# Ranks by due time instead of program place in a kernel's list scheduler (hybrid attention layer, one core)

## The chip, the cores and the metric

One core of one Trainium2 chip. The metric is device time in microseconds (us) of one execution. A kernel's engines are TensorE (PE, with its weight loads PEld), ScalarE (ACT), VectorE (DVE), GpSimd (POOL) and SyncE (SP), which issues all the DMA transfers of this kernel. Each engine works through its own list of instructions strictly in the order in which they were emitted, and waits on semaphores for what other engines or transfers have to deliver.

## The reference

One layer of a streaming encoder for two groups with the same weights: a prompt of 1024 rows and a sample of 32 rows with a cache of 512 positions. Cut to what matters:

```python
u = rmsnorm(h, g_pre) @ w_in                  # (1024, 4096): qA kA vA gA qB kB vB gB
oA = band_attention(qA, kA, vA)               # 8 heads of 64: own 64-frame chunk and 8 before, position bias, softmax
oB = stick_breaking(qB, kB, vB)               # 8 heads of 64: strictly causal
y = concat(oA * silu(gA), oB * silu(gB)) @ w_out
h = h + rmsnorm(y, g_post)
h = h + sigmoid(h @ w_ple_gate) * (p @ w_ple)
# stick_breaking:
log_1m = where(causal, log_sigmoid(-z), 0.0)
after = cumsum(log_1m, reverse=True) - log_1m
w = where(causal, exp(log_sigmoid(z) + after), 0.0)
```

The keys and values are outputs too. All is float32; matrix products are made of three products of rounded high and low parts (names ending in h and l).

## The kernel before, in words

The program is not written engine by engine. Code in program order records each instruction as an `Op` in a `Recorder` (`rec`), with its engine, its costs (`busy`: how long it occupies the engine, `late`: how long its result takes after that) and the instructions it has to come after (`after`: data, reuse of buffers). `Recorder.order` then plays a list schedule through in planned time, and `emit` writes the instructions in that order. This order is what each engine later runs; planned times themselves leave no trace on the chip. All instructions come out at one source line (L452), so the profile is read by tile names.

In `order`, the engine that is free first takes, of the instructions whose inputs are ready by then, the one with the least `key`. Keys are set in `node`: for TensorE `(cls, place in the program)`, where attention has class 0 and the projections 1 (other classes at the end); for the other four engines `(low, place in the program)`, where `low` is 0 except for a few steps (-2 and -1 for norm chains, 1 for the weight sums on GpSimd). Entries with engine "CTL" take or release buffers and cost nothing. A transfer occupies SyncE for `ISSUE`, then a common `line` for its bytes, and lands after constants; a result that goes to TensorE gets `MARGIN` more.

The stages in time:

1. Start-up (to about 40 us): x tiles are loaded, normed (`be`, `rs`), transposed on TensorE (`ptx`) into `hnh`/`hnl`, with part of the per-layer embedding product (`ple`).
2. Attention (to about 610 us): eight pairs of heads, A0, B0, A1, B1 and so on. The input projection of the next pair (`mm_qA`, `mm_kB`, ...) is woven by `weave` between scores (`SA`, `SB`), weights and values (`PVA`, `PVB`) of the present one. Scores of B go through mask (DVE), sigmoid (ACT), a scan (DVE), a difference (POOL); those of A through bias and minimum (DVE) and Exp (ACT). Weights are then transposed, mostly on TensorE (`ptwA`, `ptwB`), for two blocks of a head by a transpose on VectorE and a trip through memory: a store `swapA<-om` and four reads `be<-swapA`; then a cast to `wTh` and a subtraction to `wTl`. Keys and values go out through `ktA`, `ktB`, `vtA`, `vtB`. In the first four pairs sums of weight quarters are made for later on GpSimd (`oB`, `gB`, stored to `sum_dro`, `sum_drg`). In the last pair the eight gate projections run (`mm_gA`, `mm_gB`).
3. Output and gate projections (to the end): seven products of quarter matrices (`o0P`, `g0P`, ...) per pair of row tiles, with norm, gate and stores.

Of the kernel before, what the change touches and what calls it, by code (L numbers as in the profile page):

```python
# [8 lines left out]
F32 = mybir.dt.float32  # L9
F32R = mybir.dt.float32r  # L10
AF = mybir.ActivationFunctionType
# [161 lines left out]


class Op:
    __slots__ = ("eng", "what", "args", "kw", "key", "busy", "late", "ready", "left", "after", "at", "size", "shared")


LAND = {"PE": 165, "ACT": 0, "DVE": 0, "POOL": 0, "SP": 0, "CTL": 0}
SEM = 60  # L180
MARGIN = 400
ISSUE = 600
DMA_NS, DMA_RATE, DMA_MARGIN = 1500, 320.0, 2000
DVE_SET, POOL_SET = 137, 110


# [77 lines left out]
class Recorder:  # L264
# [35 lines left out]
    def node(self, eng, what, args, kw, after):  # L300
        o = Op()
        o.eng, o.what, o.args, o.kw, o.after = eng, what, args, kw, after
        o.key = (self.cls if eng == "PE" else self.low, len(self.ops))
        o.shared = False
        self.ops.append(o)
        return o

    def add(self, eng, what, args, kw):
        writes, reads = [], []
        method = what[1] if isinstance(what, tuple) else ""  # L310
        for i, a in enumerate(args):
            if isinstance(a, (View, Raw, Segments)):
                (writes if i == 0 or (method == "tensor_tensor_reduce" and i == 7) else reads).append(a)
        for k, a in kw.items():
            if isinstance(a, (View, Raw, Segments)):
                (writes if k in ("out", "accum_out") else reads).append(a)
        o = self.node(eng, what, args, kw, set())
        for mine, write in ((reads, False), (writes, True)):
            for v in mine:
                b = v.buf  # L320
                hit = False
                for other, box, wrote in b.uses:
                    if other is not o and (write or wrote) and all(p < y and x < q for (p, q), (x, y) in zip(v.box, box)):
                        o.after.add(other)
                        hit = True
                if b.pool is not None:
                    if not hit:
                        o.after.add(b.place)
                    b.pool.ops.append(o)
                b.uses.append((o, v.box, write))  # L330
        o.busy, o.late = self.cost(eng, method, args, kw, writes, reads)
        o.shared = eng == "POOL"
        if eng == "DVE":
            sbuf = [v for v in reads if isinstance(v, (View, Segments)) and not v.buf.psum and v.free() > 4]
            o.shared = len(sbuf) > 1 or (method == "tensor_copy" and len(sbuf) == 1 and not writes[0].buf.psum)

    @staticmethod
    def cost(eng, method, args, kw, writes, reads):

        out = writes[0] if writes else None  # L340
        n = out.free() if isinstance(out, View) else 1
        psum = any(isinstance(v, (View, Segments)) and v.buf.psum for v in reads)
        if eng == "PE":
            if method == "transpose":
                return (109 if args[1].shape[0] > 64 else 62), 165
            return max(109.0, 2.5 + 0.449 * args[2].free()) * (1 if args[2].buf.dtype == F32R else 4), 165
        if eng == "ACT":
            return (60 if psum else 95) + 0.83 * n + (190 if "accum_out" in kw else 0), 105
        if eng == "DVE":
            if method == "tensor_tensor_scan":  # L350
                return 120 + 2.1 * n, 85
            if method == "tensor_copy" and not psum:
                return 70 + 0.53 * n, 85
            if method == "scalar_tensor_tensor":
                return 125 + 1.04 * n, 85
            if method == "tensor_tensor_reduce":
                return 90 + 1.04 * n, 150
            return 70 + 1.04 * n, 85
        if eng == "POOL":
            if method == "tensor_tensor":  # L360
                if n == 1:
                    return 535, 40
                return 170 + (1.77 if out.buf.dtype == F32 else 2.15) * n, 40
            if method == "tensor_scalar":
                return 255 + 0.86 * n, 0
            return 100 + 0.82 * n, 0
        size, run = 4, 0
        for v in (out, args[1]):
            if isinstance(v, View) and v.buf.pool is not None:
                size, run = 4 * v.shape[0] * v.free(), 4 * v.shape[-1]  # L370
        return ISSUE, max(size / DMA_RATE, size / run * (8.5 + 0.0365 * run) / 16)


    def order(self):

        import heapq
        for place, old in self.turns:
            place.after.update(x[0] for x in old.uses)
        users = {id(o): [] for o in self.ops}
        for o in self.ops:  # L380
            o.left, o.ready = len(o.after), 0.0
            for a in o.after:
                users[id(a)].append(o)
        names = ("PE", "ACT", "DVE", "POOL", "SP", "CTL")
        free = dict.fromkeys(names, 0.0)
        soon = {e: [] for e in names}
        now = {e: [] for e in names}
        for o in self.ops:
            if not o.left:
                heapq.heappush(soon[o.eng], (0.0, o.key, id(o), o))  # L390
        out, port, line = [], 0.0, 0.0
        while len(out) < len(self.ops):
            best = None
            for e in names:
                if now[e]:
                    t = free[e]
                elif soon[e]:
                    t = max(free[e], soon[e][0][0])
                else:
                    continue  # L400
                if best is None or t < best[0]:
                    best = (t, e)
            t, e = best
            while soon[e] and soon[e][0][0] <= t:
                _, key, n, o = heapq.heappop(soon[e])
                heapq.heappush(now[e], (key, n, o))
            o = heapq.heappop(now[e])[2]
            if o.shared and e == "DVE" and port > t + DVE_SET:
                held = [x for x in now[e] if not x[2].shared]
                if held:  # L410
                    heapq.heappush(now[e], (o.key, id(o), o))
                    pick = min(held)
                    now[e].remove(pick)
                    heapq.heapify(now[e])
                    o = pick[2]
            o.at = t
            if e == "CTL":
                done = t
            elif e == "SP":
                free[e] = t + o.busy  # L420
                line = max(line, t + o.busy + DMA_NS) + o.late
                done = line + DMA_MARGIN
            else:
                if o.shared:
                    t = max(t, port - (DVE_SET if e == "DVE" else POOL_SET))
                    port = t + o.busy
                free[e] = t + o.busy
                done = t + o.busy + o.late
            out.append(o)
            for u in users[id(o)]:  # L430
                if u.eng == e and e != "SP":
                    r = t if e == "CTL" else free[e] if e == "PE" else done
                else:
                    r = done + (0 if u.eng == "CTL" else SEM + (MARGIN if u.eng == "PE" else 0))
                u.ready = max(u.ready, r)
                u.left -= 1
                if not u.left:
                    heapq.heappush(soon[u.eng], (u.ready, u.key, id(u), u))
        return out


    def emit(self, tc):
# [15 lines left out]
def stream_step(  # L458
# [333 lines left out]
    def attention(ab, p, h):  # L792
# [23 lines left out]
        def rooms(i):  # L816

            more = ab == "B"
            g = together.get(i, (i,))
            if g not in whole:  # L820
                n = sum(cost(x) for x in g) * P
                whole[g] = ring0.tile([P, n + more * len(g)], f"om{nm}_{i}"), ring1.tile([P, n], f"be{nm}_{i}")
            k, n = g.index(i), cost(i) * P
            a = sum(cost(x) for x in g[:k]) * P
            w0, w1 = whole[g]
            return w0[:, a + more * k:a + more * k + n + more], w1[:, a:a + n]
# [886 lines left out]
    for m, (nm, src, group) in enumerate(sets):  # L1713
        last_set = m == len(sets) - 1
        state = [{}, {}]
        for n, prod in enumerate(ORDER):
            for pair, t in enumerate(group):
# [43 lines left out]
                if nm == "o":  # L1761
                    rec.low = -1
                    if prod == "P2":
                        add(st["h1u"][:, L], st["p1"], bank, ALU.add)
                        st["u"].square(0, st["h1u"][:, L])
# [103 lines left out]
```

## Time and profile before

| | us |
|---|---|
| median of 3 runs | 804.93 |
| lowest and highest run | 804.59, 805.31 |
| profiled execution, its own time | 809.23 |
| its span, first to last instruction | 807.4 |
| VectorE busy in it | 567.9 |
| ScalarE busy in it | 504.4 |
| GpSimd busy in it | 432.1 |

The profiled execution is one single run with recording on. Its span is what the views below divide up. In a view of waits a row names the waiting engine and tile, the engine and tile it waited for, and then the total in us, the number of times and the longest. In a timeline a row gives start, duration, engine, line, operation, output<-input, and in brackets idle time before it and what ended it. SPq is SyncE's queue of transfer issues; its duration is that of the issue and not of the transfer.

### The profile page before, as it was taken

To read this page: it belongs to the slowest core of one execution; us is meant where nothing else is said; L and a number is where in the kernel's file an instruction comes from. 1 tells how busy PE (TensorE), PEld (TensorE's weight loads), DVE (VectorE), ACT (ScalarE), POOL (GpSimd) and SP (SyncE) were. 2 spreads that over 40 slices of the span, in tenths; PEclk is the share of its full clock that TensorE was granted. 3 is DMA by queue.
4 is the path that set the end of the run, shared out by engine and by line. 5 is a ranking of instruction groups with operands and counts; after the bars stand their busy time and mean duration, and the time that the engine had idled before them with its cause. 6 is when DMAs were issued, how large, how long until landed. Compare 5 with 4: busy or idle time off the path is not lost.

```text
span 807.4 us, 14271 instructions
## 1 busy us (share of the span) xinstructions
PE 788.0 (98%) x4646; PEld 722.3 (89%) x4646; DVE 567.9 (70%) x1007; ACT 504.4 (62%) x1061; POOL 432.1 (54%) x503
## 2 busy tenths in 40 slices
PE   8999989999999999999999999999999999999997
PEld 7899989899989999899999989999997777878786
DVE  7626768786588788788886688765435787477655
ACT  5636774676586646795675696543327977877641
POOL 5623655764356668134551236777542549598513
PEclk9999999999999999999999999999999999999999
DMA  8419895667878749854535667765569948869633
GB/s 276 149 45 293 215 253 175 195 185 217 225 225 246 215 121 267 216 146 133 151 81 169 147 175 212 234 199 152 166 207 322 298 147 270 278 218 302 215 108 131
DMA packets 160973, 161.09 MB, mean 199 GB/s; under 512 B 39154, under 2 KB 120794, under 8 KB 160899
## 3 DMA queue, kind: packets, MB, share of 16 engines
q1 hardware_dynamic: 160898, 160.18, 67.1%
q8 instruction: 37, 0.61, 0.3%
q14 instruction: 38, 0.30, 0.1%
HBM read 99.23 MB, written 52.49 MB: 188 GB/s over the span
## 4 chain that ended last, share of the span: by engine, by line
PE 72%; DMA 6%; ACT 6%; POOL 5%; DVE 5%; issue 4%; SPq 2%; DVEq 0%; POOLq 0%; ACTq 0%
PE mm_gA L452 6%; PE mm_gB L452 6%; PE mm_kA L452 5%; PE mm_qA L452 5%; PE mm_qB L452 4%; PE SB L452 3%; PE mm_vA L452 3%; PE PVB L452 3%; PE mm_kB L452 3%; PE PVA L452 3%; PE mm_vB L452 3%; PE SA L452 2%; PE o1P L452 2%; PE g2P L452 2%; PE g3P L452 2%
## 5 line engine op out<-in xcount | busy, mean ns | idle before, releaser
L452 POOL TENSOR_TENSOR be<-om 128x128 f32<-128x128 f32 (+7 forms) x64 | 75.4, 1184 | 64.8 <-DVE om L452 29.0
L452 DVE TENSOR_TENSOR_SCAN om<-om,SB 128x384 f32<-128x384 f32 (+5 forms) x96 | 94.9, 1001 | 9.1 <-ACT om L452 7.4
L452 ACT ACTIVATE om<-SB 128x384 f32<-128x384 f32 (+5 forms) x96 | 44.4, 493 | 36.0 <-DVE SB L452 26.9
L452 ACT ACTIVATE be<-om,statA 128x640 f32<-128x640 f32 (+3 forms) x64 | 44.4, 694 | 18.2 <-DVE statA L452 11.0
L452 DVE TENSOR_TENSOR wTl<-be,wTh 128x640 fp32r<-128x640 f32 (+1 forms) x32 | 37.6, 1175 | 10.3 <-ACT wTh L452 8.8
L452 ACT CAST wTh<-ptwB 128x512 fp32r<-128x512 f32 (+3 forms) x64 | 29.5, 481 | 19.6 <-PE ptwB L452 15.4
L452 DVE TENSOR_TENSOR wTl<-ptwB,wTh 128x512 fp32r<-128x512 f32 (+3 forms) x64 | 33.7, 545 | 10.3 <-ACT wTh L452 7.8
L452 DVE TENSOR_TENSOR wTl<-ptwA,wTh 128x512 fp32r<-128x512 f32 (+2 forms) x64 | 29.8, 483 | 15.7 <-ACT wTh L452 12.5
L452 POOL TENSOR_TENSOR oB<-oB,oB 128x256 f32<-128x256 f32 x32 | 27.7, 882 | 18.6 <-DMA oB<-in_w_out_dram 10.5
L452 DVE STREAM_TRANSPOSE om<-be 128x640 f32<-128x640 f32 (+1 forms) x32 | 28.9, 904 | 9.8 <-POOL be L452 4.9
L452 PE MATMUL SB<-kdB,LB 128*128 128x384 f32 (+5 forms) x96 | 34.0, 357 | 1.6 <-DVE om L452 1.6
L452 DVE CUSTOM_DVE_ANT_0 om<-SA,biasA 128x320 f32<-128x320 f32 (+3 forms) x64 | 29.5, 482 | 7.6 <-PE SA L452 4.4
L452 ACT CAST wTh<-ptwA 128x512 fp32r<-128x512 f32 (+2 forms) x64 | 26.2, 426 | 13.3 <-PE ptwA L452 7.5
L452 PE MATMUL SB<-klB,LB 128*128 128x384 f32 (+5 forms) x96 | 32.9, 345 | 0.0
L452 PE MATMUL SA<-kdA,LA 128*128 128x320 f32 (+2 forms) x96 | 30.2, 325 | 0.7 <-DVE LA L452 0.4
L452 POOL TENSOR_TENSOR sggA<-sggA,oggA 128x352 f32<-128x352 f32 x24 | 23.8, 991 | 11.2 <-DVE sggA L452 10.8
L452 PE MATMUL SA<-klA,LA 128*128 128x320 f32 (+2 forms) x96 | 29.6, 320 | 0.0
L452 ACT CAST wTh<-be 128x640 fp32r<-128x640 f32 (+1 forms) x32 | 25.0, 782 | 6.4 <-DMA swapA<-om 3.3
L452 PE MATMUL ptwB<-ident,be 128*128 128x128 f32 x192 | 28.7, 273 | 0.0
L452 PE MATMUL ptwA<-ident,be 128*128 128x128 f32 x160 | 26.3, 276 | 2.0 <-ACT be L452 1.8
L452 DVE TENSOR_TENSOR SB<-SB,maskb 128x128 f32<-128x128 f32 x64 | 17.3, 287 | 13.5 <-PE SB L452 13.1
L452 POOL TENSOR_TENSOR klA<-stkA,kdA 64x1024 fp32r<-64x1024 f32 x8 | 20.7, 2587 | 8.2 <-ACT kdA L452 7.7
(707 smaller groups left out, 2650.5 us busy)
## 6 DMA issues: line engine op xcount, KB each, us to landing
swapA<-om SPq DMA_DIRECT2D x16, 320.0 KB, 2.8
be<-swapA SPq DMA_DIRECT2D x64, 80.0 KB, 3.9
oB<-in_w_out_dram SPq DMA_DIRECT2D x16, 256.0 KB, 4.9
sum_dro<-oB SPq DMA_DIRECT2D x16, 256.0 KB, 3.3
gB<-in_w_ple_gate_dram SPq DMA_DIRECT2D x16, 256.0 KB, 4.6
sum_drg<-gB SPq DMA_DIRECT2D x16, 256.0 KB, 3.8
x<-in_x_prompt_dram SPq DMA_DIRECT2D x16, 256.0 KB, 5.2
h_dr<-h SPq DMA_DIRECT2D x8, 512.0 KB, 3.3
```

Of the source, the lines that this page charges most:

```text
L452: getattr(getattr(tc.nc, o.what[0]), o.what[1])(*args, **kw)
```

## The change

`order` becomes a loop over two new functions. `plan` is the old list schedule; it now also returns when its last engine is free. `due` goes backwards through a plan: each instruction's due time is the earliest of what its users allow, TensorE instructions being due at the time at which the plan before had them; an instruction without users is due at the plan's end. Outside TensorE that due time becomes the `key`. One plan with the old keys is followed by three rounds of `due` and `plan`; the last plan is emitted (two conditions are switched off by `0`). TensorE keeps its key.

The cost constants change too: one wake-up time per engine instead of one margin for TensorE, 30 ns more for most instructions of ScalarE, VectorE and GpSimd, 520 instead of 600 ns for an issue, another landing time of transfers, and 1310 ns wherever ScalarE goes from Exp to Sigmoid or back.

```diff
-MARGIN = 400
-ISSUE = 600
-DMA_NS, DMA_RATE, DMA_MARGIN = 1500, 320.0, 2000
+WAKE = {"PE": 400, "ACT": 100, "DVE": 100, "POOL": 190, "SP": 0}
+ISSUE = 520
+DMA_RATE, LANDING, WAKE_DMA = 320.0, 2500, 200
+TABLE_NS = 1310
...
+        o.table = next((a for a in args if a in (AF.Exp, AF.Sigmoid)), None) if eng == "ACT" else None
...
-            return (60 if psum else 95) + 0.83 * n + (190 if "accum_out" in kw else 0), 105
+            return (90 if psum else 125) + 0.83 * n + (190 if "accum_out" in kw else 0), 105
...
-            return 70 + 1.04 * n, 85
+            return 100 + 1.04 * n, 85
...
     def order(self):
 
-        import heapq
         for place, old in self.turns:
             place.after.update(x[0] for x in old.uses)
         users = {id(o): [] for o in self.ops}
         for o in self.ops:
-            o.left, o.ready = len(o.after), 0.0
             for a in o.after:
                 users[id(a)].append(o)
+        best, end = self.plan(users)
+        for _ in range(3):
+            self.due(best, users, end)
+            out, last = self.plan(users)
+            if last >= end and 0:
+                break
+            best, end = out, last
+        return best
+
+    def due(self, out, users, end):
+
+        late, after = {}, {}
+        for o in reversed(out):
+            e = o.eng
+            t = after.get(e, end) if 0 and e != "CTL" else end
+            for u in users[id(o)]:
+                v = late[id(u)]
+                if u.eng == e and e not in ("SP", "CTL"):
+                    v -= 0.0 if e == "PE" else o.late
+                elif u.eng != "CTL":
+                    v -= SEM + WAKE[u.eng] + (WAKE_DMA if e == "SP" and u.eng != "SP" else 0) + o.late * (e != "SP")
+                elif e != "SP":
+                    v -= o.late
+                if e == "SP":
+                    v -= LANDING + o.late
+                t = min(t, v)
+            if e == "PE":
+                late[id(o)] = o.at
+                continue
+            late[id(o)] = t - o.busy if e != "CTL" else t
+            if e != "CTL":
+                after[e] = late[id(o)]
+                o.key = (late[id(o)], o.key[1])
+
+    def plan(self, users):
...
             elif e == "SP":
                 free[e] = t + o.busy
-                line = max(line, t + o.busy + DMA_NS) + o.late
-                done = line + DMA_MARGIN
+                line = max(line, free[e]) + o.late
+                done = line + LANDING
             else:
+                if o.table and o.table != table:
+                    table = o.table
+                    t = max(free[e] + TABLE_NS, t)
...
                 else:
-                    r = done + (0 if u.eng == "CTL" else SEM + (MARGIN if u.eng == "PE" else 0))
+                    r = done + (0 if u.eng == "CTL" else SEM + WAKE[u.eng] + (WAKE_DMA if e == "SP" and u.eng != "SP" else 0))
...
-        return out
+        return out, max(free.values())
```

More of the change, by code (lines that the diff above doesn't have):

```diff
@@ L175 @@
 class Op:
-    __slots__ = ("eng", "what", "args", "kw", "key", "busy", "late", "ready", "left", "after", "at", "size", "shared")
+    __slots__ = ("eng", "what", "args", "kw", "key", "busy", "late", "ready", "left", "after", "at", "size", "shared", "table")
 LAND = {"PE": 165, "ACT": 0, "DVE": 0, "POOL": 0, "SP": 0, "CTL": 0}
 SEM = 60
-MARGIN = 400
-ISSUE = 600
-DMA_NS, DMA_RATE, DMA_MARGIN = 1500, 320.0, 2000
+WAKE = {"PE": 400, "ACT": 100, "DVE": 100, "POOL": 190, "SP": 0}
+ISSUE = 520
+DMA_RATE, LANDING, WAKE_DMA = 320.0, 2500, 200
+TABLE_NS = 1310
 DVE_SET, POOL_SET = 137, 110
@@ L303, in node @@
         o.key = (self.cls if eng == "PE" else self.low, len(self.ops))
-        o.shared = False
+        o.shared, o.table, o.busy, o.late = False, None, 0.0, 0.0
         self.ops.append(o)
@@ L347, in cost @@
         if eng == "ACT":
-            return (60 if psum else 95) + 0.83 * n + (190 if "accum_out" in kw else 0), 105
+            return (90 if psum else 125) + 0.83 * n + (190 if "accum_out" in kw else 0), 105
         if eng == "DVE":
             if method == "tensor_tensor_scan":
-                return 120 + 2.1 * n, 85
+                return 150 + 2.1 * n, 85
             if method == "tensor_copy" and not psum:
-                return 70 + 0.53 * n, 85
+                return 100 + 0.53 * n, 85
             if method == "scalar_tensor_tensor":
-                return 125 + 1.04 * n, 85
+                return 155 + 1.04 * n, 85
             if method == "tensor_tensor_reduce":
-                return 90 + 1.04 * n, 150
-            return 70 + 1.04 * n, 85
+                return 120 + 1.04 * n, 150
+            return 100 + 1.04 * n, 85
         if eng == "POOL":
@@ L361, in cost @@
                 if n == 1:
-                    return 535, 40
-                return 170 + (1.77 if out.buf.dtype == F32 else 2.15) * n, 40
+                    return 565, 40
+                return 200 + (1.77 if out.buf.dtype == F32 else 2.15) * n, 40
             if method == "tensor_scalar":
@@ L380, in order @@
         for o in self.ops:
-            o.left, o.ready = len(o.after), 0.0
             for a in o.after:
                 users[id(a)].append(o)
+        best, end = self.plan(users)
[30 more added lines that the diff above has]
+    def plan(self, users):
+        import heapq
+        for o in self.ops:
+            o.left, o.ready = len(o.after), 0.0
         names = ("PE", "ACT", "DVE", "POOL", "SP", "CTL")
@@ L390, in order @@
                 heapq.heappush(soon[o.eng], (0.0, o.key, id(o), o))
-        out, port, line = [], 0.0, 0.0
+        out, port, line, table = [], 0.0, 0.0, None
         while len(out) < len(self.ops):
```

## The prediction

> **What bounds the kernel now.** I read the page's busy times first, then who TensorE (PE) waited for, then stretches around its worst wait, then SyncE's queue there.
>
> ```profile
> span 807.4 us, 14271 instructions
> PE 788.0 (98%) x4646; PEld 722.3 (89%) x4646; DVE 567.9 (70%) x1007; ACT 504.4 (62%) x1061; POOL 432.1 (54%) x503
> ...
> PE PVA L452 <- ACT wTh L452: 2.7, 1, 2.7
> PE ptx L452 <- DVE be L452: 2.4, 2, 1.3
> PE ptwA L452 <- ACT be L452: 1.8, 2, 1.3
> PE SB L452 <- DVE om L452: 1.6, 3, 0.9
> PE idle L452 <- DVE newh L452: 1.3, 1, 1.3
> PE ptkA L452 <- DVE wTl L452: 1.3, 1, 1.3
> PE ptx L452 <- DVE hnl L452: 0.5, 1, 0.5
> PE o0P L452 <- ACT A12o L452: 0.5, 1, 0.5
> ...
> PE g0P L452 <- DMA hh<-h_dr: 0.3, 1, 0.3
> ...
> 100.00:104.00 4.00, 1.35 (x9) 1.05 (x7) 0.24 (x1) 0.70 (x3) 2.65 (x3) 1.00 0.91 268
> 104.00:108.00 4.00, 3.92 (x14) 3.72 (x15) 3.11 (x4) 4.00 (x10) 1.74 (x5) 0.57 1.04 243
> 780.00:808.00 28.00, 22.48 (x109) 18.64 (x108) 13.80 (x23) 5.03 (x9) 6.46 (x5) 0.99 0.31 104
> ```
>
> TensorE is busy 788.0 of 807.4 us, so it is the bound, and an order of instructions can only touch the other 19.4 us. Of these, 1.3 us lie ahead of the first matmul (idle waiting for newh, the start-up), and the last stretch shows 28.00 - 22.48 = 5.5 us without a matmul, of which 0.6 lie behind the span's end: a tail of 4.9 us. About 13.2 us are left in the middle. The window rows read: stretch, busy time of PE, weight loads, DVE, ACT, POOL, then granted clock, DMA share and GB/s. The 2.7 us wait for wTh is followed by a stretch at clock 0.57, which costs (1 - 0.57) x 4.00 = 1.7 us of TensorE work more. So 13.2 + 1.7 = 14.9 us is all that a better order could win short of head and tail.
>
> The Trainium skill, page "TensorE: Matmul & The Clock Gate", section "Part 1: The HAM clock gate", says the clock halves after about one idle window of 3.4 us. By that figure a gap of 2.7 us would leave the clock alone and step A below would be worth 2.7 instead of 4.4, which gives 800.5 us; the row of 0.57 disagrees, and the row decides.
>
> Where that wait comes from is in SyncE's queue and in the ScalarE instruction that stood for it:
>
> ```profile
> 82.86 1.29 SPq L452 DMA_DIRECT2D swapA<-om  x1
> ...
> 88.03 0.47 SPq L452 DMA_DIRECT2D kdB<-kdB  x1
> 88.59 0.55 SPq L452 DMA_DIRECT2D out_dram<-ktB  x1
> 89.23 1.00 SPq L452 DMA_DIRECT2D out_dram<-vtA  x1
> 90.33 1.71 SPq L452 DMA_DIRECT2D klB<-klB  x1
> 92.09 3.06 SPq L452 DMA_DIRECT2D out_dram<-ktB  x3
> 95.20 0.94 SPq L452 DMA_DIRECT2D be<-swapA  x1
> 96.23 0.70 SPq L452 DMA_DIRECT2D oB<-in_w_out_dram  x1
> 96.98 0.43 SPq L452 DMA_DIRECT2D sum_dro<-oB  x1
> 97.46 0.96 SPq L452 DMA_DIRECT2D be<-swapA  x2
> ...
> 99.04 0.58 SPq L452 DMA_DIRECT2D be<-swapA  x1
> ...
> 103.31 0.72 ACT L452 CAST wTh<-be 128x640 fp32r<-128x640 f32 x1 [3.30 <-DMA swapA<-om]
> ```
>
> The block of weights was stored at 82.86, but the four reads that bring it back turned go out at 95.20 to 99.04, behind five output stores (ktB, vtA), two key copies and the traffic of the weight sums. Rank in the old plan is the place in the program (`key = (low, index)`), and these were written earlier. The cast starts at 103.31, and TensorE stands. The releaser is named swapA<-om, but the queue shows that the reads were late.
>
> **The change part by part.** No instruction is added or removed, and TensorE's own rank is untouched, so the 788.0 us stay. What changes is the order on ScalarE, VectorE, GpSimd and SyncE, and through the plan's ready times which ready matmul TensorE is given next.
>
> *A, due times on SyncE.* The reads be<-swapA have a user chain cast, subtract, PVA, whose due time is the matmul's time in the pass before. The output stores of ktB and vtA have none but the reuse of their buffer, or the end of the plan. The reads pass the seven transfers at 88.03 to 92.09 and the two of the sums at 96.23 and 96.98. What they pass: kdB and klB feed scores and have early due times themselves, so they may stay ahead; the five stores alone took 0.55 + 1.00 + 3.06 = 4.6 us of the queue, and the sum's two 0.70 + 0.43 = 1.1, together 5.7 us, more than the 2.7 of the wait. Behind the moved stores wait only later users of their buffer. I take the wait and its slow clock away: -4.4 (bounds 0 and -4.4).
>
> *B, due times on the compute engines.* Three waits inside the attention are of engines that did something else first: ptwA 1.8, SB 1.6, ptkA 1.3, together 4.7. The largest of ptwA is this:
>
> ```profile
> 472.30 1.28 ACT L452 ACT_TABLE_LOAD   x1
> 473.60 0.94 ACT L452 ACTIVATE om<-SB 128x128 f32<-128x128 f32 x3
> 474.55 1.28 ACT L452 ACT_TABLE_LOAD   x1
> 475.85 0.83 ACT L452 ACTIVATE be<-om,statA 128x640 f32<-128x640 f32 x1
> ```
>
> Sigmoids for the next head were put ahead of an exponential that the transposes waited for, with two table loads of 1.28 us that the old plan did not know. The new plan charges 1.31 for each and ranks the exponential by its due time. But it does not avoid a load, it only counts it, and both may be due closely. I take half: -2.3 (bounds 0 and -4.7).
>
> *C, start-up.* ptx 2.4 and 0.5, total 2.9. The chain to these transposes runs over ScalarE's square, GpSimd's root and VectorE's scaling of tiles that have just been loaded; how much of it is queue and how much transfer the wait rows do not tell, so I take a quarter, -0.7 (bounds +1.3, one more wait as long as the longest there, and -2.9). The rows of the last stage (o0P 0.5) and the tail I leave: after the last matmul the same chain of additions, gate and store has to run.
>
> *D, the new constants.* Each ScalarE, VectorE and GpSimd instruction counts 30 ns more, the wake-ups 100 to 190 ns more; this spreads the plan and costs nothing on the chip by itself. The allowance for a transfer shrinks. For 256 KB (0.82 at the plan's 320 bytes per ns) the old plan had 0.60 + 1.50 + 0.82 + 2.00 + 0.06 = 5.0 us from issue to user, the new one 0.52 + 0.82 + 2.50 + 0.26 = 4.1. Against that, issue to landing:
>
> ```profile
> be<-swapA SPq DMA_DIRECT2D x64, 80.0 KB, 3.9
> oB<-in_w_out_dram SPq DMA_DIRECT2D x16, 256.0 KB, 4.9
> raw<-sum_drg SPq DMA_DIRECT2D x16, 256.0 KB, 4.4
> hh<-h_dr SPq DMA_DIRECT2D x16, 256.0 KB, 4.6
> raw<-in_w_ple_gate_dram SPq DMA_DIRECT2D x12, 256.0 KB, 5.3
> wr_gA<-in_w_in_dram SPq DMA_DIRECT2D x8, 256.0 KB, 6.1
> ```
>
> All five groups of 256 KB land later than 4.1, only two later than 5.0. A user planned at 4.1 stands at the head of its engine with everything behind it. The read-backs of 80 KB (0.26) have 0.52 + 0.26 + 2.50 + 0.26 = 3.5 instead of 4.4, against 3.9 measured. What hides this is that loads are fetched ahead into spare buffers: TensorE's only direct wait for a transfer above is g0P's 0.3. I charge one new wait of the size that stands three times above, +1.3 (bounds 0 and the rival below).
>
> The Trainium skill, page "DMA: Bandwidth & Descriptors", section "Latency and other measured facts", speaks against this edit: memory latency is 0.2 us on average and 2 us at high load, so one fixed allowance fits no loaded stretch. The rows from 4.4 to 6.1 for one size agree.
>
> Sum: -4.4 - 2.3 - 0.7 + 1.3 = -6.1. The profiled execution took 809.23 (span 807.4 and 1.8 around it), so it would take 803.1. The median of the runs, 804.93, lies 4.3 under the profiled one; I keep that distance: 798.8.
>
> **The rivals.**
> *Transfers planned too early (slower).* The five groups are 68 loads, over 4.1 by 0.8, 0.3, 0.5, 1.2 and 2.0, a weighted mean of 0.82 us. Where the user's engine stands that long and TensorE has no other ready matmul in its fixed order, the whole 0.82 is lost. If a third of them (23) do so: +18.9, less the 7.4 won in A to C: +11.5, 816.4. It decides from 7.4 / 0.82 = 9 such loads. For it: the rows above. Against it: g0P's 0.3 us, the only direct wait, although two groups were later than the old allowance too.
>
> *TensorE's order goes wrong (slower).* Ranks come from the TensorE times of the pass before, and the last of the passes is kept even if an earlier one ended sooner. If attention chains finish sooner, TensorE takes them first and the projection that should fill the next pair's start is used differently. One more wait of 1.3, as at ptwA or ptkA, in each of eight pairs is 10.4; with the 6.1 won, +4.3: 809.2. It decides from five such waits. For it: 98% busy leaves every new gap visible. Against it: ranks that reproduce TensorE's last times pull each pass towards the one before.
>
> *Nothing measurable.* The wait at 101 goes and others of the same sum come, as on chains whose length and not whose queue is late: 804.9.
>
> *All waits go (faster, stronger).* 14.9 less: 790.0.
>
> **How the numbers follow.** About 0.2% (1.6 us) is what a measurement can tell from no change. My forecast with its stronger form 0.57 (some 0.10 of it near 790); nothing measurable 0.06; transfers too early 0.19; TensorE's order 0.18. The likeliest time is 798.8, its own range 793 to 803. For 8 in 10 the range has to take in the bound of 790 and the first slower rival to 816.4, so 790 to 817; the rest is beyond either end. Faster 0.57, same 0.06, slower 0.37.
>
> **What would show it.** A: reads be<-swapA follow their store within some 4 us, output stores stand behind them, no wait of PVA over 2 us, and clock 1.00 in all stretches after the start. B: fewer ScalarE and VectorE entries in PE's waits, ptwA below 1. C: ptx below 2.4. D: PE's and ACT's waits for DMA stay under 2 us in all. PE stays at 788 +- 2 and its idle falls from 19.4 to about 15. It is wrong if waits for DMA rise on ACT, DVE and POOL with PE idle above 19, or if PE's idle collects in the first 50 us or at a pair's start.

## The result, and the profile after

The changed kernel takes 798.89 us (median of 4 runs, 796.26 to 800.65) against 804.76 for the kernel before (804.44 to 805.31): ratio 0.9922, 95% interval 0.9898 to 0.9945. The gain is 5.9 us; the prediction said 6.1 and 798.8.

The two profiled executions are further apart than that: 809.23 and 796.26, with spans of 807.4 and 794.2. The first lies 4.5 us above the median of its kernel, and the second is the fastest of the change's four runs. The difference of this pair of profiles is therefore not the gain; where I compare below, I take a second profile of the kernel before (span 805.2, first experiment) beside the first, and the profile of a close variant of the change (the first nudge, span 797.9) beside the change's.

TensorE's totals and waits after, then its busy time in three stretches (columns as in the prediction):

```profile
span 794.2 us, 14262 instructions
...
PE 781.9 (98%) x4646; PEld 723.1 (91%) x4646; DVE 572.6 (72%) x1007; ACT 503.8 (63%) x1061; POOL 438.9 (55%) x503
...
PE ptwA L494 <- ACT sumrowA L494: 2.7, 1, 2.7
PE idle L494 <- DVE newh L494: 1.3, 1, 1.3
PE SA L494 <- DMA klA<-klA: 1.1, 1, 1.1
PE SsB L494 <- DVE QsB L494: 0.5, 1, 0.5
PE pth L494 <- DVE wlS4o L494: 0.4, 1, 0.4
PE ple L494 <- ACT wph1True L494: 0.4, 1, 0.4
PE o2P L494 <- DVE h L494: 0.3, 1, 0.3
PE ptx L494 <- DVE be L494: 0.3, 1, 0.3
...
0.00:125.00 125.00, 119.04 (x730) 111.66 (x731) 78.70 (x153) 75.76 (x160) 62.62 (x96) 1.00 0.69 202
125.00:600.00 475.00, 474.37 (x3053) 461.08 (x3052) 360.72 (x648) 296.20 (x637) 266.92 (x303) 1.00 0.68 194
600.00:780.00 180.00, 179.23 (x816) 142.40 (x815) 125.30 (x194) 129.24 (x262) 104.26 (x100) 1.00 0.69 230
```

The same stretches in the first profile of before:

```profile
0.00:125.00 125.00, 117.42 (x720) 110.21 (x720) 76.91 (x149) 74.83 (x156) 61.15 (x96) 0.99 0.70 203
125.00:600.00 475.00, 468.90 (x2995) 450.65 (x2994) 353.02 (x638) 291.13 (x624) 259.63 (x301) 1.00 0.66 187
600.00:780.00 180.00, 179.18 (x829) 142.77 (x828) 124.11 (x198) 133.36 (x272) 104.87 (x102) 1.00 0.76 245
```

What to see: the number of matmuls is the same (4646). Between 125 and 600 us, the attention, TensorE was idle for 475.00 - 468.90 = 6.1 us and is now idle for 0.6, and gets 3053 instead of 2995 matmuls done in the same time. Up to 125 us the idle time fell only from 7.6 to 6.0. From 600 to 780 us it stayed at 0.8. The three waits of step B (ptwA <- be, SB <- om, ptkA <- wTl) are gone from the list.

The queue around the read-backs, SyncE's timeline:

```profile
81.46 0.34 SPq L494 DMA_DIRECT2D swapA<-om  x1
...
87.20 3.80 SPq L494 DMA_DIRECT2D out_dram<-ktB  x4
91.05 2.50 SPq L494 DMA_DIRECT2D be<-swapA  x4
93.66 0.47 SPq L494 DMA_DIRECT2D kdB<-kdB  x1
94.17 0.59 SPq L494 DMA_DIRECT2D out_dram<-vtA  x1
...
97.18 0.58 SPq L494 DMA_DIRECT2D sum_dro<-oB  x1
```

The four reads now go out at 91.05 in one piece, ahead of kdB, vtA and the sums, where they were spread over 95.20 to 99.04 before. But the four stores of ktB are still ahead of them, and the reads still come 9.6 us after their store (95.20 - 82.86 = 12.3 before).

### The profile page after: what moved, and what is told of

The parts are those of the page before. It is cut to its first block, busy times and chain, and to the rows that moved or that the text cites. A ratio compares the mean times of both kernels' runs of the same rounds, so it can differ in the third digit from the quotient of the medians.

```text
span 794.2 us, 14262 instructions
## 1 busy us (share of the span) xinstructions
PE 781.9 (98%) x4646; PEld 723.1 (91%) x4646; DVE 572.6 (72%) x1007; ACT 503.8 (63%) x1061; POOL 438.9 (55%) x503
## 4 chain that ended last, share of the span: by engine, by line
PE 91%; DMA 2%; DVE 2%; POOL 2%; issue 1%; ACT 1%; SPq 1%; DVEq 0%; ACTq 0%; POOLq 0%
PE mm_gB L494 6%; PE mm_gA L494 6%; PE mm_qB L494 6%; PE mm_kB L494 6%; PE mm_vA L494 5%; PE mm_kA L494 5%; PE mm_vB L494 5%; PE mm_qA L494 5%; PE PVB L494 4%; PE SB L494 4%; PE SA L494 4%; PE PVA L494 4%; PE ptwB L494 3%; PE g0P L494 2%; PE g1P L494 2%; PE o1P L494 2%
## 5 line engine op out<-in xcount | busy, mean ns | idle before, releaser
L494 POOL TENSOR_TENSOR be<-om 128x384 f32<-128x384 f32 (+7 forms) x64 | 79.0, 1241 | 64.7 <-DVE om L494 38.8
L494 ACT ACTIVATE be<-om,statA 128x640 f32<-128x640 f32 (+4 forms) x64 | 44.5, 696 | 10.1 <-DVE statA L494 6.5
L494 DVE TENSOR_TENSOR wTl<-be,wTh 128x640 fp32r<-128x640 f32 (+1 forms) x32 | 35.3, 1105 | 4.7 <-ACT wTh L494 4.3
L494 DVE CUSTOM_DVE_ANT_0 om<-SA,biasA 128x320 f32<-128x320 f32 (+2 forms) x64 | 29.7, 483 | 9.0 <-PE SA L494 8.3
L494 POOL TENSOR_TENSOR oB<-oB,oB 128x256 f32<-128x256 f32 x32 | 24.2, 777 | 13.8 <-DMA oB<-in_w_out_dram 12.5
L494 POOL TENSOR_TENSOR gB<-gB,gB 128x256 f32<-128x256 f32 x32 | 26.0, 832 | 6.8 <-DMA gB<-in_w_ple_gate_dram 6.7
```

The source lines that it names most:

```text
L494: getattr(getattr(tc.nc, o.what[0]), o.what[1])(*args, **kw)
```

## The experiments

All ratios are to the kernel before, run beside on the same chip, with 95% intervals. The ratio is the record's and not the quotient of two medians; below the first row, the kernel before had medians of 805.07 (beside the rows from "before, again" to "ranks on SyncE alone"), 806.37 (beside the two nudges and the last two rows) and 805.52 (beside the others). One profile belongs to each kernel, so a single wait in it is one execution's. The last column is the mean of the granted TensorE clocks that the runs of the row recorded; those of the kernel before beside them had 0.9978 to 0.9986.

| kernel | median us | ratio | interval | clock |
|---|---|---|---|---|
| the change | 798.89 | 0.9922 | 0.9898 to 0.9945 | 0.9980 |
| before, again | 805.83 | 1.0005 | 0.9986 to 1.0023 | 0.9981 |
| ranks by due time, all old constants | 807.89 | 1.0038 | 1.0022 to 1.0054 | 0.9954 |
| new constants, ranks by place | 807.35 | 1.0024 | 1.0007 to 1.0041 | 0.9946 |
| ranks on SyncE alone | 803.50 | 0.9996 | 0.9977 to 1.0014 | 0.9960 |
| ranks on ACT, DVE, POOL alone | 807.01 | 1.0014 | 0.9996 to 1.0033 | 0.9965 |
| no table loads in the plan | 806.77 | 1.0016 | 1.0000 to 1.0032 | 0.9967 |
| old engine costs | 804.92 | 0.9990 | 0.9971 to 1.0009 | 0.9985 |
| semaphore 64 ns (nudge) | 799.95 | 0.9923 | 0.9900 to 0.9946 | 0.9982 |
| landing 2560 ns (nudge) | 801.56 | 0.9949 | 0.9931 to 0.9968 | 0.9988 |
| old transfer allowance | 794.77 | 0.9880 | 0.9852 to 0.9907 | 0.9990 |
| old transfer allowance, issue 520 ns | 810.32 | 1.0047 | 1.0029 to 1.0064 | 0.9945 |
| old transfer allowance, ranks by place | 812.82 | 1.0083 | 1.0064 to 1.0102 | 0.9952 |

**The kernel before, a second profile.** No edit.

> The kernel before once more, unchanged, to see what of its profile is its own and what belongs to one execution. If the waits of its first profile are systematic, the profile shows PVA waiting 2 to 3 us for wTh near 101 us, a stretch at half clock behind it, and PE idle of about 19 us. If the 2.7 us wait and the slow clock (4.4 us together) belong to that execution alone, the span is near 803 us, PE's longest wait is under 2 us and the clock is 1.00 throughout; then step A of the prediction is not what the change removed. The time is 804.8 +- 0.5 either way.

```profile
span 805.2 us, 14271 instructions
...
PE ptwA L452 <- DVE wTl L452: 2.3, 1, 2.3
PE ptwA L452 <- ACT be L452: 1.8, 2, 1.3
PE SB L452 <- DVE om L452: 1.6, 3, 1.0
...
PE ptkA L452 <- DVE wTl L452: 1.3, 1, 1.3
...
PE ptx L452 <- DVE be L452: 0.7, 1, 0.7
...
117.00:121.00 4.00, 4.00 (x17) 3.90 (x16) 3.95 (x6) 2.33 (x7) 3.45 (x6) 0.57 0.63 199
...
107.10 2.27 SPq L452 DMA_DIRECT2D be<-swapA  x4
...
113.80 0.72 ACT L452 CAST wTh<-be 128x640 fp32r<-128x640 f32 x1 [2.82 <-DMA be<-swapA]
...
116.16 0.91 PE L452 MATMUL ptwA<-ident,be 128*128 128x128 f32 x5 [2.33 <-DVE wTl L452]
```

Neither outcome as written; the median, 805.83, lies outside 804.8 +- 0.5 too. The waits of the compute engines return to the tenth (ptwA 1.8, SB 1.6, ptkA 1.3): they belong to the order. The 2.7 us of PVA does not return (0.3 here); in its place ptwA waits 2.3 us for wTl, again with a stretch at 0.57 behind it. The cause is of the same kind, one block later: ScalarE stood 2.82 us at the cast that waits for the next read-backs, and what ptwA needed came behind that cast. So in both profiles one wait of more than 2 us comes between 100 and 120 us, where ScalarE stands for read-backs; which block and which matmul it meets differed.

**Ranks without the new constants, and the constants without ranks.**

```diff
# ranks alone: all constants of before, and
-                if o.table and o.table != table:
+                if 0 and o.table and o.table != table:
# constants alone:
-        for _ in range(3):
+        for _ in range(0):
```

> Due times as ranks in three rounds, with all cost constants of the kernel before. If the ranks carry the gain of 5.9 us: 799 +- 1.5. If the new constants carry it: 804 to 806. If the shorter transfer allowance costs something: below 797.

> The new constants, with ranks by program place on all engines (no round of due times). If the ranks carry the gain: 804 to 808 (the shorter transfer allowance without better ranks rather costs). If a plan closer to the chip carries it: 798 to 801.

Each half alone is slower than before, by 0.4% and 0.2%. The constants alone came out at 807.35, in the range given for the ranks as carrier, but the ranks alone at 807.89, outside all three of theirs: no half carries the gain of the change by itself. Both halves also ran at a lower mean clock, by 0.003 and 0.004. Over 805 us that is an estimated 2.6 and 3.2 us, about as much as their medians lie above 805.07, so stretches at half clock behind their waits may be most of what they lose.

**Ranks on one kind of engine.**

```diff
-                o.key = (late[id(o)], o.key[1])
+                if e == "SP":     # the other run: if e != "SP":
+                    o.key = (late[id(o)], o.key[1])
```

> The change with due times as ranks on SyncE alone; ScalarE, VectorE and GpSimd keep the program's place. If the read-backs that go ahead of output stores carry it (step A, 4.4 of the predicted 7.4): 799 to 801. If the compute engines' ranks carry it: 803 to 806.

> The change with due times as ranks on ScalarE, VectorE and GpSimd alone; SyncE keeps the program's place. The mirror of the run with ranks on SyncE alone, which came out at no difference. If the compute engines' ranks carry the gain: ratio to before 0.991 to 0.995 (797 to 801). If both are needed because a transfer that is issued late undoes a well ranked chain: 0.997 to 1.002 (803 to 807).

Neither differs from before. The second is what its expectation gave for "both are needed" (0.997 to 1.002); the first, at 803.50, lies in the range for the compute engines as carrier, which the second does not bear out. The stretches say why, first with ranks on SyncE alone, then on the three compute engines alone:

```profile
0.00:125.00 125.00, 117.94 (x732) 110.41 (x733) 76.58 (x151) 75.54 (x159) 60.42 (x96) 1.00 0.70 203
125.00:600.00 475.00, 469.68 (x3021) 455.50 (x3020) 360.22 (x643) 289.88 (x627) 263.33 (x302) 1.00 0.68 191
```

```profile
PE ptwA L495 <- ACT sumrowA L495: 4.9, 2, 4.4
...
111.75 1.88 SPq L495 DMA_DIRECT2D be<-swapA  x4
...
117.25 0.72 ACT L495 CAST wTh<-be 128x640 fp32r<-128x640 f32 x1 [4.71 <-DMA be<-swapA]
...
118.35 0.25 ACT L495 COPY sumrowA<-ptsA 8x128 f32<-8x128 f32 x1
...
0.00:125.00 125.00, 114.52 (x696) 107.71 (x697) 70.25 (x145) 73.95 (x154) 60.34 (x94) 0.99 0.68 198
125.00:600.00 475.00, 472.47 (x3040) 458.18 (x3039) 360.44 (x647) 292.00 (x629) 266.88 (x304) 1.00 0.67 191
```

Idle TensorE in the two stretches, against 7.6 and 6.1 in the first profile of before: 7.1 and 5.3 with SyncE's ranks, 10.5 and 2.5 with the compute engines'. The compute engines' ranks do repair the attention, but with SyncE in the program's order they lose nearly as much in the first 125 us, where one wait alone took 4.4 us. The row names a small copy to sumrowA, but that copy only stood third in ScalarE's list: ScalarE waited 4.71 us at the cast before it, for read-backs that SyncE issued at 111.75. With both, 6.0 and 0.6. That is what these profiles show for the two ranks needing one another; one profile of each is not more than an indication of size.

**Table loads and engine costs taken out of the plan.**

```diff
# no tables
-                if o.table and o.table != table:
+                if 0 and o.table and o.table != table:
# old engine costs: cost() as before, and
-WAKE = {"PE": 400, "ACT": 100, "DVE": 100, "POOL": 190, "SP": 0}
+WAKE = {"PE": 400, "ACT": 0, "DVE": 0, "POOL": 0, "SP": 0}
```

> The change with table loads not counted by the plan; all else as changed. If counting them removes the wait of ptwA for an exponential near 475 us (1.4 us in both profiles of before) and others like it: 1.5 to 3 us slower than the change, ratio 0.994 to 0.997, and a wait ptwA <- be over 1 us is back. If it is the ranks that removed it: 0.991 to 0.993 and no such wait.

> The change with the old costs of ScalarE, VectorE and GpSimd instructions (30 ns less each) and without their wake-ups; transfers and table loads as changed. Ranks with all old constants were slower than before, so some constant carries it. If it is these (chains of small waits in the plan that is otherwise too quick): ratio 0.998 to 1.004. If it is the transfers' or tables' constants: 0.991 to 0.995.

Both lose the gain, the first by more than was expected (1.0016, not 0.994 to 0.997), the second within the range given for the engine costs as carrier. But the mechanism I had named is not the one: without table loads in the plan no wait of ptwA for the exponential came back, and ScalarE even loads tables less often (8 against 10):

```profile
PE ptwA L494 <- ACT sumrowA L494: 3.0, 2, 2.1
...
L494 ACT ACT_TABLE_LOAD x8 | 10.3, 1283 | 0.8 <-PEq L1899 0.7
```

Other waits took its place. This raised the doubt that any touch of the constants draws another plan, and that the change was a lucky draw.

**Two neutral nudges.** `SEM = 64` for 60, and 2560 for 2500 in the landing.

> The change with 64 instead of 60 ns for a semaphore in the plan: a neutral nudge that makes no rule better or worse. If the gain belongs to the parts of the change: ratio 0.990 to 0.995, as the change. If every nudge of a constant draws another plan and its waits scatter by several us (each ablation so far came out between 0.999 and 1.004, whatever it took away): anywhere in 0.988 to 1.004, and the gain is partly this one plan's.

> The change with 2560 instead of 2500 ns for a landing: a second neutral nudge. By the parts of the change: 0.990 to 0.995. By scatter: another value than the first nudge, anywhere in 0.988 to 1.004.

0.9923 and 0.9949: the gain survives both of these nudges, so it is not the luck of a single plan. Yet its size scatters by some 0.3%, and the profiles show the parts moving: idle of 5.4 and 2.9 us in the two stretches of the first nudge, 5.5 and 5.8 in the second.

```profile
0.00:125.00 125.00, 119.63 (x725) 111.65 (x726) 76.04 (x151) 75.94 (x158) 63.34 (x95) 0.99 0.69 201
125.00:600.00 475.00, 472.14 (x3040) 458.26 (x3039) 368.38 (x647) 292.45 (x630) 267.24 (x303) 1.00 0.68 192
```

**The transfers' allowance.**

```diff
-ISSUE = 520
+ISSUE = 600                                # stays 520 in the second run
-DMA_RATE, LANDING, WAKE_DMA = 320.0, 2500, 200
+DMA_NS, DMA_RATE, LANDING, WAKE_DMA = 1500, 320.0, 2000, 0
-                    v -= LANDING + o.late
+                    v -= DMA_NS + LANDING + o.late
-                line = max(line, free[e]) + o.late
+                line = max(line, free[e] + DMA_NS) + o.late
# third run: the first, with
-        for _ in range(3):
+        for _ in range(0):
```

> The change with the transfers' old model: issue 600 ns, 1500 ns ahead of the line, 2000 ns behind it, no wake-up; engine costs, wake-ups and table loads stay new. By the first rival of the prediction the shorter allowance costs up to 0.8 us per late load, so the old one is faster: ratio 0.985 to 0.991. If the shorter allowance is what lets SyncE's planned queue keep up with the real one: 0.997 to 1.003. If it matters little: 0.991 to 0.994.

> The old transfer allowance of the kernel that came out at 0.988, but with 520 ns for an issue as in the change. If the longer landing makes the difference (late loads no longer stop an engine's list): 0.986 to 0.990 again. If the longer issue does (SyncE's planned queue as slow as the real one): 0.991 to 0.995. If 0.988 was one lucky plan: 0.992 to 1.003.

> The kernel with the old transfer allowance and the other new constants, but with ranks by program place on all engines. If ranks by due time are what gains and the allowance only keeps it: 0.998 to 1.004, as the constants alone. If the engine costs and table loads do it once the transfers are not planned too early: 0.988 to 0.994.

The first is the fastest kernel of this study, 0.9880; its interval and the change's overlap a little, so that it beats the change is not shown. With the same constants and ranks by place the third is 1.0083, outside both of its ranges, so here the ranks are worth 2.0%, and with the changed constants 1.0% (0.9922 against 1.0024); with all old constants they lost 0.4%. What lies between that loss (1.0038) and 0.9880 is the engine costs, the wake-ups and the table loads alone, which agrees with the two runs that took one of them out. But the second run warns against reading such steps as prices. It falls outside all three of its ranges: 80 ns less for an issue turn 0.9880 into 1.0047. Its profile shows what it lost by, not why the plan fell that way:

```profile
PE PVB L494 <- DVE v2B L494: 3.3, 1, 3.3
PE ptwA L494 <- DVE wTl L494: 2.8, 2, 2.5
...
146.30 5.09 DVE L494 TENSOR_TENSOR v2B<-vtB,v2B 128x512 fp32r<-128x512 f32 x1
...
144.41 1.89 POOL L494 TENSOR_TENSOR be<-om 128x1024 f32<-128x1024 f32 x1
146.26 2.38 POOL L494 TENSOR_TENSOR klA<-stkA,kdA 64x1024 fp32r<-64x1024 f32 x1
...
148.71 1.25 POOL L494 TENSOR_TENSOR wl_vA<-wr_vA,wh_vA 128x512 fp32r<-128x512 f32 x1
...
150.12 0.71 POOL L494 TENSOR_TENSOR oB<-oB,oB 128x256 f32<-128x256 f32 x1
```

A subtraction on VectorE took 5.09 us while GpSimd had one two-input operation after the other, and ended 0.56 us after the last of them; PVB waited 3.3 us for it. This kernel's clock, 0.9945, is the lowest of the table. Whether the landing, the issue or such a meeting makes the difference of the allowances stays open. A ratio of one plan is not the worth of the constant that was turned: the nudges moved it by 0.3%, this step of 80 ns by 1.7%.

## Why the prediction was right, and where

The time and the direction hold; the terms of the sum do not all. That the median was met to 0.1 us is luck: errors cancelled, and the sum was built on the waits of one profiled execution, for which it forecast 803.1 after the change. The change's profiled execution took 796.26; that pair differs by 13.0 us, the medians by 5.9.

What came of the steps shows in TensorE's idle time by stretches, in us, in the two profiles of before, the change's, and that of the first nudge (profiled at 799.85, its median 799.95):

| | before | before, again | the change | first nudge |
|---|---|---|---|---|
| 0 to 50 us (start-up, step C) | 4.4 | 3.7 | 2.1 | 2.5 |
| 50 to 125 us (read-backs, step A) | 3.2 | 3.2 | 3.9 | 2.9 |
| 125 to 600 us (attention, step B) | 6.1 | 5.2 | 0.6 | 2.9 |
| PE busy in all | 788.0 | 787.3 | 781.9 | 783.9 |

*The bound* held in part. Head and tail stayed (1.3 and 4.9 us), and idle TensorE in the middle shrank: in all it fell from 19.4 to 12.3, where about 15 was forecast. But "the 788.0 us stay" failed: 781.9, and 783.9 in the nudge. In the change's profile 1.7 of it is the slow clock, which that execution did not have; the nudge's had it. The rest I had not seen. The page calls a matmul's modelled end its end, so records overlap:

```profile
L452 PE MATMUL mm_kB<-hnh,wl_kB 128*128 128x352 f32 x96 | 20.2, 330 | 0.0
```

These 96 records of 330 ns are 31.7 us long together and fill 20.2, so a short wait hides inside busy time. An estimate from the starts of all matmuls fits. For each pair that follow one another I took how much later the second starts than in the quickest quarter of pairs of their sizes. Outside gaps and slow clock this sums to 59.3 and 59.1 us in the profiles of before, 53.9 in the change's and 55.4 in the nudge's. The bound of 14.9 us was too small by such hidden waits.

*A*, 4.4, came to nothing as far as the profiles show. The reads do go out earlier and undivided, and PVA's wait is gone; but TensorE's idle time from 50 to 125 us went from 3.2 to 3.9. The rows are those of before and of the change, then the wait that took the place:

```profile
50.00:125.00 75.00, 71.78 (x452) 69.34 (x450) 44.97 (x97) 46.60 (x99) 35.95 (x45) 0.98 0.78 215
50.00:125.00 75.00, 71.10 (x455) 68.80 (x455) 47.66 (x101) 47.28 (x103) 37.73 (x45) 1.00 0.75 213
...
111.22 0.26 ACT L494 COPY sumrowA<-ptsA 8x128 f32<-8x128 f32 x1 [3.66 <-DMA o_dr<-otA]
```

ScalarE now stood 3.66 us for the store of otA, with which sumrowA shares two buffers, and TensorE 2.7 behind it. The wait that was priced was one execution's: in the second profile of before the reads went out as late (93.69 to 97.22) and PVA waited 0.3. Nor does the slow clock's 1.7 stand as a gain: the change's four runs had a mean clock of 0.9980, the ten of before again 0.9981, and the nudge has its stretch at half clock too. And the stores of ktB are not put behind: "reads follow their store within some 4 us" was wrong by 5.6 us at that place.

*B*, 2.3, was right or too small. All three waits went, 4.7, and idle TensorE in the attention fell by 5.5 in the change's profile, by 3.2 and 0.3 in those of the nudges (each about 1 less against the second profile of before). These waits were in both profiles of before to the tenth, that of step A was not. That is the difference I ought to have weighed: in these two profiles the waits on a chain of engines repeated, and the wait at a crowded transfer queue fell elsewhere.

*C*, 0.7, was too small: ptx fell from 2.9 to 0.3 (1.4 in the second profile of before), and idle TensorE up to 50 us by 2.3 or 1.7. The whole decline up to 125 us is C's.

*D*, +1.3: one new wait for a transfer came, SA for klA, 1.1. Two figures of this step were off: the allowance of 4.1 us leaves out the user's wake-up of 0.10 to 0.19, and the sign that waits of PE and ACT for transfers stay under 2 us in all was met neither after (3.66 at sumrowA alone) nor before (3.30 at the cast alone). The rival that transfers are planned too early is not shown: the longer allowance was faster in one plan and slower in its neighbour. The rival of TensorE's order did not come about with the change, but runs with ranks and other constants (1.0038, 1.0047) show that a slower result was near.

The step that failed is A's: its price was read from one execution, and another transfer's wait stood in its place, so the idle time that its 4.4 us stood for did not fall. The term that made up for it was put at nothing: TensorE's busy time, which fell by 3.4 to 6.1 us in these pairs. One profile of each kernel is an indication of these sizes and no more.

## What to carry to other kernels

Ranks by due time pay when every engine has them, the transfer queue too, and when the plan's costs fit: each half alone gained nothing here. In a kernel whose bound engine is 98% busy, take a second profile before pricing a wait: those that return to the tenth are the order's, and what stands behind a transfer may move and be replaced by the next. When a wait names an instruction, look at what its engine did just before: twice here ScalarE stood for read-backs, and TensorE's row named something behind them. And before an ablation of a planner's constant is read as that constant's worth, run a neutral nudge: here it moved the result by 0.3%, and a change of 80 ns once by 1.7%.

## What the runs showed of the hardware

TensorE's clock fell to half behind waits of 2.3 and 2.7 us in the two profiles of before and stayed up behind one of 2.7 in the change. In the first nudge it fell behind two waits of 0.9 and 1.0 us that came within 3 us of each other:

```profile
110.40 0.66 PE L494 MATMUL ptwA<-ident,be 128*128 128x128 f32 x4 [0.93 <-ACT sumrowA L494]
112.09 0.33 PE L494 MATMUL ptwA<-ident,be 128*128 128x128 f32 x1 [1.03 <-DVE wTl L494]
...
112.00:116.00 4.00, 3.91 (x15) 3.91 (x16) 3.84 (x7) 2.12 (x3) 2.45 (x2) 0.57 0.72 197
```

So a wait's length alone did not decide. The Trainium skill, page "TensorE: Matmul & The Clock Gate", section "Part 1: The HAM clock gate", has the clock follow how busy TensorE was in a window of about 3.4 us that is free-running. A window that does not start with the wait would fit a fall behind one wait and none behind another of the same length, but no run here varied it.

A two-input operation of VectorE that takes 0.66 us where GpSimd rests (the one at 152.87 us) took 5.09 us next to GpSimd's. The Trainium skill, page "SBUF — State Buffer", section "🔬 SBUF: two separate sides", says that such an operation and GpSimd's lock a shared pair of ports for a whole instruction, whoever starts first; the rows fit that, and VectorE stood through more than one of GpSimd's instructions. The fastest of these subtractions in the same kernel:

```profile
L494 DVE TENSOR_TENSOR v2B<-vtB,v2B x8: 660/792/5091, 146.3 to 510.7; 128x512 fp32r<-128x512 f32 x8
```
